# Spacing the transpose banks, moving the sample scores, the first value casts and the last row transposes

## The chip, the cores and the metric

The kernel runs on one core of a Trainium2 chip. The metric is the device time of one execution in microseconds (us). The profile is one execution of the kernel, recorded instruction by instruction; its times are microseconds from the start of the span, which runs from the first to the last instruction.

The engines are named as in the profile: PE is TensorE (matrix multiplications and transposes), DVE is VectorE, ACT is ScalarE, POOL is GpSimd and SP is SyncE, which issues nearly all DMA transfers here.

## What is computed

One step of a decoder layer is computed for 256 new prompt tokens and 8 x 8 sample tokens, 320 columns in all, at a width of 2048: a mixing part (convolution and RWKV-7), then cross-attention into 256 memory tokens, then a gated feed-forward part. The change touches the attention and the very end of the feed-forward part. Cut to these, the reference is:

```python
    h = rms_norm(x, p['norm_xa_pre'])
    q = (h @ p['w_q']).reshape(b_, t_, XA_HEADS, XA_HEAD_DIM)        # 4 heads of 512
    s = jnp.einsum('bthd,bmhd->bhtm', q, mem_k.astype(q.dtype)).astype(jnp.float32) * (XA_HEAD_DIM ** -0.5)
    attn = jax.nn.softmax(s, axis=-1).astype(x.dtype)
    o = jnp.einsum('bhtm,bmhd->bthd', attn, mem_v.astype(x.dtype)).reshape(b_, t_, XA_HEADS * XA_HEAD_DIM)
    x = x + rms_norm(o @ p['w_o'], p['norm_xa_post'])
    ...                                                              # feed-forward, ending in w_down
```

The prompt uses one set of memory keys and values (computed earlier in the kernel), and each of the 8 sample sequences uses its own from a cache: per head, 9 key tiles and 9 value tiles of 256 x 512 float32.

## The kernel before

Products are kept near float32 by splitting each float32 operand into a high and a low float16 part and multiplying three pairs. For each weight tile (`raw`, 512 KB by DMA) ACT makes the high part (`whi`, line 154), DVE the low part (`wlo`, line 155), and PE multiplies (line 57: results `acc`, 128 x 320). A new tile is loaded into one of three `raw` buffers, and there are three `whi` and three `wlo`.

In the attention the kernel works head by head, in two code streams, one for the prompt and one for the samples, which advance between the matmuls of the query weights `w_q` (16 output blocks, four for each head) and of the first columns of the output weights `w_o`:

- A memory tile is loaded into one of five buffers (`rawkv`, line 1176). Keys have to be transposed: PE turns 128 x 128 blocks, four into a PSUM bank (`pk`, line 61), ACT casts the bank to the high part `kh` (line 1245), DVE makes the low part `kl` (line 1246). Values need no transposition: ACT casts the whole tile to `vh` (line 1259), DVE makes `vl` (line 1260).
- The queries leave PSUM on DVE (`qf`, line 1206); ACT and DVE split the prompt's part (`qp`), and ACT and POOL split the samples' part (`qs`, lines 1208, 1211 and 1212).
- The sample scores `pss` use 32-column pieces: four matmuls of 32 columns run side by side on PE, one for each of four sequences. The same is done for the sample outputs `pos`. The prompt's scores and outputs are `psc` and `pav`.
- The softmax takes a maximum on DVE (line 1268), an exponential on ACT (`e`, line 1272), a reciprocal and a scaling on DVE (lines 1273 and 1275). The weights are then turned on PE: `pat` for the prompt, `pas` for the samples; the sample outputs are turned as `pot`.

All of `pk`, `pat`, `pas` and `pot` take a PSUM bank from one group of three (tag `m`), each of which has to be read out by ACT and DVE before it is used again.

What sets the order: the code streams say `yield x` to wait until a planned clock has advanced by x us. That clock is a sum of the planned times of the PE instructions written so far (`mm`, `turn`). So the order is written by the plan, and then a scheduler with its own model of the engines, and priorities, orders each engine's instructions. Loads of memory tiles have a higher priority than the rest of the attention. On the chip every engine runs its instructions in that order and waits on semaphores for what the others have to deliver. The DMA issues on SP stand in one queue in the same way: a load that waits for a buffer holds back the loads behind it.

At the end of the kernel (lines 1540 to 1600) the `w_down` output blocks are scaled on DVE into `mtf` (line 1552) and turned on PE to rows (`pmt`, line 61), while the last `w_down` columns are multiplied from tiles that are held in SBUF (the loop over `held`).

Of the kernel before, what the change touches and what calls it, by code (L numbers as in the profile page):

```python
# [9 lines left out]
F32 = mybir.dt.float32  # L10
# [26 lines left out]
PRI = 3000  # L37
LAT = 1.2
CLAT = 20.0
TAPLAT = 1.18  # L40
KBUF = 8
VBUF = 4
# [4 lines left out]
def hybrid_step_kernel(ctx: ExitStack, tc: tile.TileContext, I, O):  # L47
# [4 lines left out]
    ring = ctx.enter_context(tc.tile_pool(name="ring", bufs=1))  # L52

    clock, pe = [0.0], [None]

    def mm(out, lhsT, rhs, start, stop, skip=False, share=1):
        pe[0] = TE.matmul(out, lhsT=lhsT, rhs=rhs, start=start, stop=stop, skip_group_check=skip)  # L57
        clock[0] += math.prod(rhs.shape[1:]) * (4 if rhs.dtype == F32 else 1) / (2400.0 * share)

    def turn(out, in_, idn):  # L60
        pe[0] = TE.transpose(out, in_, idn)  # L61
        clock[0] += in_.shape[0] / 1200.0

    def late(ins):
        tc.add_manual_dep(ins.ins, pe[0].ins.name, mybir.DependencyInfo(mybir.DependencyClass.NoSync, mybir.DependencyReason.DATA), reason="late")


    ident = cst.tile([P, P], F32, name="ident")
# [1163 lines left out]
    def key_tiles(srcs, h):  # L1232
        t_ = yield from room("k", len(srcs))
        tiles = [[atk.tile([P, 4, NPR], F16, tag=g, bufs=KBUF, name=g) for g in ("kh", "kl")] for _ in srcs]
        raws = [early.pop(n) if n in early else load_kv(src, h, not started) for n, src in srcs]
        started.append(1)
        for raw, (kh, kl) in zip(raws, tiles):
            for z in range(2):
                px = psB.tile([P, 512], F32, tag="m", bufs=3, name="pk")
                for d in range(2):  # L1240
                    for m in range(2):
                        dc = m * 512 + (2 * z + d) * P
                        turn(px[:, d * 256 + m * P:d * 256 + (m + 1) * P], raw[:, dc:dc + P], ident)
                pv = px.rearrange("p (d m) -> p d m", m=NPR)
                A.activation(kh[:, 2 * z:2 * z + 2], pv, AF.Copy, scale=SX)
                V.scalar_tensor_tensor(kl[:, 2 * z:2 * z + 2], pv, SX, kh[:, 2 * z:2 * z + 2], ALU.mult, ALU.subtract)
                yield 0.6
        return tiles, t_

    def value_tiles(srcs, h, kind="v"):  # L1250
        t_ = yield from room(kind, len(srcs))
        tiles = []
        for src in srcs:
            raw = load_kv(src, h)
            if kind == "v":
                vh, vl = (at.tile([P, RING], F16, tag=g, bufs=VBUF, name=g) for g in ("vh", "vl"))
            else:
                vh, vl = (atk.tile([P, 4, NPR], F16, tag=g, bufs=KBUF, name=g).rearrange("p d m -> p (d m)") for g in ("kh", "kl"))
            A.activation(vh, raw, AF.Copy, scale=SX)  # L1259
            V.scalar_tensor_tensor(vl, raw, SX, vh, ALU.mult, ALU.subtract)  # L1260
            tiles.append((vh, vl))
            yield 1
        return tiles, t_

    def softmax(pv, n):

        s = at.tile([P, 4, 2], F32, tag="sst", bufs=2, name="sst")
        V.tensor_reduce(s[:, 0, 0:n], pv, AX.X, ALU.max)
        V.tensor_scalar(s[:, 1, 0:n], s[:, 0, 0:n], -SCL, None, ALU.mult)
        e = at.tile([P, 2, NPR], F32, tag="e", bufs=2, name="e")  # L1270
        for j in range(n):
            A.activation(e[:, j], pv[:, j], AF.Exp, bias=s[:, 1, j:j + 1], scale=SCL, accum_out=s[:, 2, j:j + 1])
        V.reciprocal(s[:, 3, 0:n], s[:, 2, 0:n])
        for j in range(n):
            V.tensor_scalar(e[:, j], e[:, j], s[:, 3, j:j + 1], SA, ALU.mult, ALU.mult)
        return e

    def acc_bank(name):
        return psB.tile([P, 512], F32, tag="acc", name=name)

    def prompt_attention(h):
# [11 lines left out]
        e = softmax(px.rearrange("p (t m) -> p t m", m=NPR), 2)  # L1293
        ((vh, vl),), tv_ = yield from value_tiles([VO], h, "k" if h == 3 else "v")
        yield 3.02
        px = psB.tile([P, 512], F32, tag="m", bufs=3, name="pat")
        for m in range(2):
            for tt in range(2):
# [34 lines left out]
        t_[0] = True  # L1333

    def sample_weights(e, ats):
        px = psB.tile([P, 512], F32, tag="m", bufs=3, name="pas")
        for m in range(2):
            turn(px[:, m * P:(m + 1) * P], e[:, 0, m * P:(m + 1) * P], ident)
        for m in range(2):
            pv = px[:, m * P:(m + 1) * P].rearrange("p (j r) -> p j r", j=4)[:, :, 0:16].rearrange("p j (b e) -> p j b e", b=2)  # L1340
            dh, dl = (ats[:, z, m].rearrange("p j (b e) -> p j b e", e=40)[:, :, :, 0:8] for z in range(2))
            A.activation(dh, pv, AF.Copy)
            V.tensor_tensor(dl, pv, dh, ALU.subtract)
# [11 lines left out]
    def sample_out(h, pos):  # L1355
        os_ = at.tile([P, 512], F32, tag="os", bufs=1, name="os_")
        A.activation(os_, pos, AF.Copy, scale=1.0 / SA)
        yield 0.92
        while oops[h // 2] is None:
            yield 0.5  # L1360
        px = psB.tile([P, 512], F32, tag="m", bufs=3, name="pot")
        for d in range(4):
            turn(px[:, d * P:(d + 1) * P], os_[:, d * P:(d + 1) * P], ident)
        for d in range(4):
            pv = px[:, d * P:(d + 1) * P].rearrange("p (j r) -> p j r", j=4)[:, :, 0:16]
            f = 4 * (h % 2) + d
            dh, dl = (oops[h // 2][:, f, z, 256:320].rearrange("p (j r) -> p j r", j=4) for z in range(2))
            A.activation(dh, pv, AF.Copy)
            V.tensor_tensor(dl, pv, dh, ALU.subtract)
        adone[h] += 1  # L1370
# [14 lines left out]
    def sample_attention():  # L1385
# [4 lines left out]
        for h in range(4):  # L1390
            while qdone[0] < 4 * h + 4:
                yield 0.5
            yield 1.45
            pss = acc_bank("pss")
            sample_scores(h, 0, pss, *kts[h, 0])
            yield 0.21
# [6 lines left out]
            sw_ = spawn(vtiles(h, 1, "k")) if h == 3 else None  # L1403
            kn = spawn(knext(h + 1)) if h < 3 else None
            yield 4.92
            sample_weights(e, atw[h % 2])
            yield 2.2
            (vt,) = yield from join(sv_)
            pos = acc_bank("pos")
# [137 lines left out]
    gpost = vD["norm_ffn_post"]  # L1547
    pt_ = {}

    def turned(f, mi, acc):  # L1550
        z = bw.tile([P, T], F32, tag="qf", name="mtf")
        V.tensor_scalar(z, acc[:, :T], gpost[:, f:f + 1], INV, ALU.mult, ALU.mult)
        for j in range(3):
            if mi == 0:
                pt_[j] = psB.tile([P, 512], F32, tag="m", bufs=3, name="pmt")
            turn(pt_[j][:rows[j], mi * P:(mi + 1) * P], z[:, j * P:j * P + rows[j]], ident)
            if mi == 3 and f < KD - 1:
                A.activation(mtok[j][:, (f - 3) * P:(f + 1) * P], pt_[j][:rows[j]], AF.Copy)

    for _ in project(I["w_down"][0], KF, opn(act), turned, sums[:, 2], (0, 4, 8, 12, 15)):  # L1560
        pass
# [10 lines left out]
    for js, c0, c1 in (((1, 2), P, T), ((0,), 0, P)):  # L1572
        acc = psB.tile([P, 512], F32, tag="acc", name="acc")
        n = c1 - c0
        for kt, ((hi, lo), k) in enumerate(held):
            kc = slice(k * P, (k + 1) * P)
            mm(acc[:, :n], hi[:, kc], act[:, kt, 0, c0:c1], kt == 0, False)
            mm(acc[:, :n], hi[:, kc], act[:, kt, 1, c0:c1], False, False)
            mm(acc[:, :n], lo[:, kc], act[:, kt, 0, c0:c1], False, kt == KF - 1)
# [61 lines left out]
```

## Time and profile before

| quantity | value |
| --- | --- |
| median of 3 runs | 2090.84 us (2090.81 to 2093.16) |
| the profiled execution's own time | 2092.7 us |
| its span, first to last instruction | 2090.9 us |
| mean granted TensorE clock | 0.989 |
| PE busy | 2007.5 us (96% of the span) |
| DVE, ACT, POOL busy | 1396.2, 992.6, 591.9 us |

The profiled execution's time is 1.8 us more than its span, and 1.9 us more than the median. Each row of the profile that names an instruction gives its start, its duration, engine, source line, the operation with what it writes and reads, shape and count; in brackets stands how long the engine sat idle just before, and whose completion ended that. The attention of this section lies between about 871 and 1121 us.

### The profile page before, as it was taken

The numbers are of one execution on the slowest core, as the hardware profiler recorded it, in microseconds if no ns is written. First come the engines' busy times: TensorE is split into PE (matmuls) and PEld (weight loads), VectorE is DVE, ScalarE is ACT, GpSimd is POOL, SyncE is SP. The second block draws the span as 40 slices with busy tenths as digits, with TensorE's granted clock in tenths as the row PEclk, the third lists the DMA queues.
The fourth block names the chain that finished last, engine by engine and source line by source line (L and its number), as shares of the span: only waits on it lengthen the run. The fifth ranks groups of instructions, "written<-read, shape, count | busy, mean of one in ns | idle before, by whom it ended". The sixth has DMA issues, their size and how long they took to land.

```text
span 2090.9 us, 44949 instructions
## 1 busy us (share of the span) xinstructions
PE 2007.5 (96%) x17941; PEld 1393.0 (67%) x17941; DVE 1396.2 (67%) x2479; ACT 992.6 (47%) x1710; POOL 591.9 (28%) x908
## 2 busy tenths in 40 slices
PE   8989999898899999989999999999999999999998
PEld 6756666565454576566677667777777777777777
DVE  5698787986876635977774596666666666444344
ACT  5444445344545544756663454444444444533332
POOL 3635436344022111300001242444444444000000
PEclk9999999999999999999999999999999999999999
DMA  6543334332546765767775445555555555555554
GB/s 188 149 117 101 85 99 112 98 95 65 155 135 208 232 211 176 237 211 243 249 231 162 143 136 163 163 162 163 163 162 162 162 162 162 147 161 162 154 147 144
DMA packets 301998, 333.34 MB, mean 159 GB/s; under 512 B 33882, under 2 KB 227237, under 8 KB 301764
## 3 DMA queue, kind: packets, MB, share of 16 engines
q1 hardware_dynamic: 301788, 330.46, 52.6%
q8 instruction: 141, 2.31, 0.4%
q14 instruction: 69, 0.57, 0.1%
HBM read 319.90 MB, written 11.22 MB: 158 GB/s over the span
## 4 chain that ended last, share of the span: by engine, by line
PE 74%; DVE 11%; DMA 7%; ACT 3%; issue 3%; POOL 2%; SPq 0%; DVEq 0%; POOLq 0%; ACTq 0%
PE acc L57 59%; PE acck L57 5%; DVE wlo L155 3%; DMA rawkv<-in_cache_mem_v_dram 2%; PE pX L57 1%; DVE cvmix L821 1%; ACT whi L154 1%; DVE vl L1260 1%; DMA out_dram<-fo 1%; DMA raw<-in_w_v_dram 1%; PE pk L61 1%; DMA rawkv<-out_dram 1%; DMA raw<-in_w_k_dram 1%; DVE xr L1141 1%; PE psX L57 1%
## 5 line engine op out<-in xcount | busy, mean ns | idle before, releaser
L57 PE MATMUL acc<-h,whi 128*128 128x320 f16 (+1 forms) x4736 | 979.9, 301 | 11.7 <-DVE h L1143 3.7
L155 DVE SCALAR_TENSOR_TENSOR wlo<-raw,whi 128x1024 f16<-128x1024 f32 (+1 forms) x512 | 627.5, 1228 | 473.3 <-ACT whi L154 467.7
L57 PEld LDWEIGHTS <-whi 128*128 128x128 f16 (+1 forms) x7080 | 685.6, 99 | 277.5 <-issue 16.3
L154 ACT ACTIVATE whi<-raw 128x1024 f16<-128x1024 f32 (+1 forms) x512 | 533.0, 1043 | 599.6 <-PE acc L57 497.6
L57 PE MATMUL acc<-h,wlo 128*128 128x320 f16 (+1 forms) x2368 | 701.2, 300 | 0.2 <-DVE wlo L155 0.2
L57 PEld LDWEIGHTS <-wlo 128*128 128x128 f16 (+1 forms) x3540 | 348.4, 98 | 142.4 <-issue 7.1
L57 PE MATMUL acc<-act,whi 128*128 128x320 f16 x1320 | 270.3, 299 | 0.0
L57 PE MATMUL acc<-act,wlo 128*128 128x320 f16 x660 | 196.3, 299 | 0.0
L57 PE MATMUL acck<-whi,memo 128*128 128x512 f16 x512 | 152.6, 383 | 1.3 <-ACT memo L942 1.3
L821 DVE SCALAR_TENSOR_TENSOR cvmix<-GX,cdw,cvmix 128x320 f32<-128x320 f32 x240 | 140.7, 586 | 2.2
L1490 POOL COPY nF<-U 128x9 f32<-128x9 f32 x88 | 50.3, 571 | 302.3 <-DVE U L1489 299.4
L57 PEld LDWEIGHTS <-memo 128*128 128x128 f16 x768 | 72.9, 99 | 83.0 <-issue 4.4
L1487 POOL COPY U<-stF 128x16 f32<-128x16 f32 x88 | 125.9, 1436 | 0.8 <-ACT stF L1475 0.8
L1125 POOL TENSOR_TENSOR sums<-sums,bsq 128x320 f32<-128x320 f32 x33 | 37.9, 1149 | 241.3 <-ACT bsq L1119 239.6
L57 PE MATMUL acck<-wlo,memo 128*128 128x512 f16 x256 | 96.3, 382 | 0.3 <-DVE wlo L155 0.3
L1495 DVE SCALAR_TENSOR_TENSOR C<-U,fdw,C 128x336 f32<-128x336 f32 x176 | 91.8, 564 | 0.0
L1493 ACT ACTIVATE C<-U,fdw 128x336 f32<-128x336 f32 x88 | 56.0, 660 | 34.8 <-DVE U L1489 34.8
L1488 DVE TENSOR_TENSOR U<-acc,rs 128x256 f32<-128x256 f32 x88 | 36.9, 420 | 39.5 <-PE acc L57 39.5
L1260 DVE SCALAR_TENSOR_TENSOR vl<-rawkv,vh 128x1024 f16<-128x1024 f32 x31 | 37.2, 1223 | 30.0 <-ACT vh L1259 29.9
L1211 POOL CAST qs<-qf 128x64 f16<-128x64 f32 x16 | 10.0, 623 | 161.1 <-ACT qf L1208 161.1
L57 PE MATMUL acc<-oopb,whi 128*128 128x320 f16 x256 | 53.7, 299 | 1.0 <-DVE oopb L191 1.0
L57 PE MATMUL acc<-cvmix,whi 128*128 128x320 f16 x256 | 52.1, 299 | 1.5 <-ACT memo L942 1.5
(466 smaller groups left out, 2519.4 us busy)
## 6 DMA issues: line engine op xcount, KB each, us to landing
raw<-in_w_up_dram SPq DMA_DIRECT2D x352, 256.0 KB
raw<-in_w_down_dram SPq DMA_DIRECT2D x71, 512.0 KB
raw<-in_w_in_dram SPq DMA_DIRECT2D x52, 512.0 KB
raw<-in_w_in_dram SPq DMA_DIRECT2D x64, 256.0 KB
raw<-in_w_k_dram SPq DMA_DIRECT2D x32, 512.0 KB
raw<-in_w_v_dram SPq DMA_DIRECT2D x32, 512.0 KB
raw<-in_w_out_dram SPq DMA_DIRECT2D x32, 512.0 KB
rawkv<-in_cache_mem_k_dram SPq DMA_DIRECT2D x32, 512.0 KB
```

What stands on the lines that cost most here:

```text
L57: pe[0] = TE.matmul(out, lhsT=lhsT, rhs=rhs, start=start, stop=stop, skip_group_check=skip)
L61: pe[0] = TE.transpose(out, in_, idn)
L154: A.activation(hi[:, :n], raw[:, :n], AF.Copy, scale=SW)
L155: V.scalar_tensor_tensor(lo[:, :n], raw[:, :n], SW, hi[:, :n], ALU.mult, ALU.subtract)
L821: late(V.scalar_tensor_tensor(o_, i_, cdw[:, c, j:j + 1], o_, ALU.mult, ALU.add))
L1125: (V if f > 11 else G).tensor_tensor(ssum, ssum, sq, ALU.add)
L1260: V.scalar_tensor_tensor(vl, raw, SX, vh, ALU.mult, ALU.subtract)
L1487: G.tensor_copy(us[:, :, 0:2], stF[:, :, :, j])
L1488: V.tensor_tensor(U[:, 2:258], acc[:, 0:256], rf[:, 0:256], ALU.mult)
L1490: G.tensor_copy(nF[:, :, 0, j], U[:, 256:338:10])
L1493: A.activation(c, U[:, 0:336], AF.Identity, bias=fdw[:, 3, j:j + 1], scale=fdw[:, 0, j:j + 1])
L1495: V.scalar_tensor_tensor(c, U[:, t_:t_ + 336], fdw[:, t_, j:j + 1], c, ALU.mult, ALU.add)
```

## The change

There are four edits.

1. A function `bank()` and a number `BANKLAT = 0.9`: a stream that is about to take a bank of the group of three for `pk`, `pat`, `pas` or `pot` waits until the planned clock is 0.9 us beyond the last such use.
2. The sample scores of a head wait 3.6 instead of 1.45 us of the planned clock behind the head's last query block.
3. The casts `vh` of head 0 may not stand ahead of the matmul that was written 24 matmuls earlier. This is a rule on the order alone; no semaphore goes with it.
4. The row transposes of output blocks 13 and 14 of `w_down` are put on a list, and written when the loop over the held tiles is at tile 14.

```diff
+BANKLAT = 0.9
...
+    past_pe = []
     def mm(out, lhsT, rhs, start, stop, skip=False, share=1):
+        past_pe.append(pe[0])
         pe[0] = TE.matmul(out, lhsT=lhsT, rhs=rhs, start=start, stop=stop, skip_group_check=skip)
...
-    def late(ins):
-        tc.add_manual_dep(ins.ins, pe[0].ins.name, mybir.DependencyInfo(mybir.DependencyClass.NoSync, mybir.DependencyReason.DATA), reason="late")
+    def late(ins, n=0):
+        tc.add_manual_dep(ins.ins, (past_pe[-n] if n else pe[0]).ins.name, mybir.DependencyInfo(mybir.DependencyClass.NoSync, mybir.DependencyReason.DATA), reason="late")
...
             for z in range(2):
+                yield from bank()
                 px = psB.tile([P, 512], F32, tag="m", bufs=3, name="pk")
...
-            A.activation(vh, raw, AF.Copy, scale=SX)
+            cast = A.activation(vh, raw, AF.Copy, scale=SX)
+            if h == 0:
+                late(cast, 24)
...
+    bank_at = [0.0]
+
+    def bank():
+        while clock[0] < bank_at[0]:
+            yield bank_at[0] - clock[0] + 0.01
+        bank_at[0] = clock[0] + BANKLAT
...
         yield 3.02
+        yield from bank()
         px = psB.tile([P, 512], F32, tag="m", bufs=3, name="pat")
...
     def sample_weights(e, ats):
+        yield from bank()
         px = psB.tile([P, 512], F32, tag="m", bufs=3, name="pas")
...
+        yield from bank()
         px = psB.tile([P, 512], F32, tag="m", bufs=3, name="pot")
...
-            yield 1.45
+            yield 3.6
             pss = acc_bank("pss")
...
-            sample_weights(e, atw[h % 2])
+            yield from sample_weights(e, atw[h % 2])
...
     def turned(f, mi, acc):
         z = bw.tile([P, T], F32, tag="qf", name="mtf")
         V.tensor_scalar(z, acc[:, :T], gpost[:, f:f + 1], INV, ALU.mult, ALU.mult)
-        for j in range(3):
...
+        def turn_rows():
+            for j in range(3):
...
+        if f < 13:
+            turn_rows()
+        else:
+            waiting.append(turn_rows)
...
             if kt == 14:
+                while waiting:
+                    waiting.pop(0)()
```

The order on ACT at the start of the attention: `vh<-rawkv` are the casts of the first memory values, `whi<-raw` those of the query weights. Before:

```order
L1259 ACTIVATE vh<-rawkv 128x1024
L154 ACTIVATE whi<-raw 128x1024 x3
L1259 ACTIVATE vh<-rawkv 128x1024 x2
L154 ACTIVATE whi<-raw 128x1024 x3
L1259 ACTIVATE vh<-rawkv 128x1024
```

After (the lines of the changed kernel are numbered 3 or 4 higher here):

```order
L157 ACTIVATE whi<-raw 128x1024 x7
L193 ACTIVATE qp<-qf 128x256
L1211 ACTIVATE qf<-qf 128x64
L193 ACTIVATE qp<-qf 128x256
L157 ACTIVATE whi<-raw 128x1024
```

Four value casts stood between the query weight casts, and now none does; the first `vh` stands behind the first head's `kh`.

The order on PE where the sample scores of head 1 begin: `acc<-h,whi` and `acc<-h,wlo` are the last matmuls of the head's query weights, `pss` the scores, `qs` the samples' queries. Before:

```order
L57 MATMUL acc<-h_11283,whi 128x320
L57 LDWEIGHTS wlo
L57 MATMUL acc<-h_11283,wlo 128x320
L57 LDWEIGHTS qs_9806
L57 MATMUL pss<-kh,qs_9806 32x256
```

After, with the matmuls of the query weights 49 rows further up, ahead of 11 `pk` and 19 `pav`, of which these are the last:

```order
L64 MATMUL pk<-ident,rawkv 128x128
L60 LDWEIGHTS vh
L60 MATMUL pav<-al,vh 128x256
L60 LDWEIGHTS vh
L60 MATMUL pav<-al,vh 128x256
L60 LDWEIGHTS qs_9806
L60 MATMUL pss<-kh,qs_9806 32x256
```

The scores followed the query weights at once, and now key transposes and prompt outputs of head 0 stand between.

The order on PE between the end of head 0 and head 1, where turned key blocks (`pk`), prompt weights (`pat`) and sample outputs (`pot`) take the banks. Before:

```order
L57 MATMUL acc<-h_11283,wlo 128x320
L61 MATMUL pk<-ident,rawkv 128x128 x4
L61 MATMUL pot<-ident,os__12326 128x128 x4
L61 MATMUL pk<-ident,rawkv 128x128 x8
L61 MATMUL pat<-ident,e 128x128 x4
L61 MATMUL pk<-ident,rawkv 128x128 x4
L57 LDWEIGHTS vh
L57 MATMUL pav<-ah,vh 128x256
```

After:

```order
L64 MATMUL pk<-ident,rawkv 128x128 x8
L60 LDWEIGHTS ats_9807
L60 MATMUL pos<-vl,ats_9807 32x512
L64 MATMUL pk<-ident,rawkv 128x128
L60 LDWEIGHTS ats_9807
L60 MATMUL pos<-vh,ats_9807 32x512
L64 MATMUL pk<-ident,rawkv 128x128
L60 LDWEIGHTS ats_9807
L60 MATMUL pos<-vh,ats_9807 32x512
L64 MATMUL pk<-ident,rawkv 128x128
```

Six banks were filled in a row, 24 transposes without anything between; now sample outputs stand singly between the transposes.

## Rows read from the trace of the kernel before

**Rows 1.** The page: busy time of the engines, and the chain that ended last.

```profile
PE 2007.5 (96%) x17941; PEld 1393.0 (67%) x17941; DVE 1396.2 (67%) x2479; ACT 992.6 (47%) x1710; POOL 591.9 (28%) x908
...
PE 74%; DVE 11%; DMA 7%; ACT 3%; issue 3%; POOL 2%; SPq 0%; DVEq 0%; POOLq 0%; ACTq 0%
```

**Rows 2.** Waits of PE, 873 to 1121 us: total us, times, longest us.

```profile
PE acc L57 <- ACT whi L154: 2.6, 1, 2.6
PE acc L57 <- DVE qf L1206: 2.3, 1, 2.3
PE pk L61 <- DVE kl L1246: 2.2, 4, 0.5
PE pss L57 <- DVE qf L1206: 1.9, 2, 0.9
...
PE pss L57 <- POOL qs L1211: 1.6, 2, 0.8
PE acc L57 <- DVE oopb L191: 1.0, 1, 1.0
```

**Rows 3.** Timeline of ACT: start, us, instruction, [idle before it and what ended it].

```profile
897.07 1.06 ACT L1259 ACTIVATE vh<-rawkv 128x1024 f16<-128x1024 f32 x1 [6.71 <-DMA rawkv<-in_cache_mem_v_dram]
898.04 2.93 ACT L154 ACTIVATE whi<-raw 128x1024 f16<-128x1024 f32 x3
```

**Rows 4.** The chain that ended last, 880 to 912 us: start, us, what.

```profile
885.62 3.62 DMA rawkv<-in_cache_mem_v_dram
...
891.96 5.09 DMA rawkv<-in_cache_mem_v_dram
```

**Rows 5.** Timeline of PE, start of the sample scores of head 1.

```profile
963.03 0.40 PE L57 MATMUL pss<-kh,qs 128*32 128x256 f16 x8 [0.94 <-DVE qf L1206]
```

**Rows 6.** Stretches: length, busy (x instructions) by engine, PEclk, DMA share, GB/s.

```profile
944.00:946.00 2.00, 1.31 (x8) 0.83 (x8) 1.57 (x5) 1.46 (x5) 0.00 (x0) 1.00 1.09 358
...
966.00:968.00 2.00, 2.00 (x39) 1.37 (x31) 0.92 (x1) 2.00 (x4) 0.00 (x0) 0.50 0.91 312
968.00:970.00 2.00, 2.00 (x26) 1.12 (x24) 2.00 (x4) 0.51 (x2) 0.00 (x0) 0.67 0.40 129
...
1022.00:1024.00 2.00, 2.00 (x37) 0.94 (x31) 1.87 (x3) 1.56 (x4) 0.00 (x0) 0.51 0.58 203
1042.00:1076.00 34.00, 34.00 (x345) 25.56 (x345) 29.14 (x41) 24.16 (x41) 4.37 (x7) 1.00 0.99 326
```

**Rows 7.** Timeline of PE, turned blocks between heads 0 and 1.

```profile
943.99 0.66 PE L61 MATMUL pk<-ident,rawkv 128*128 128x128 f32 x4 [0.54 <-DVE kl L1246]
944.87 0.66 PE L61 MATMUL pat<-ident,e 128*128 128x128 f32 x4 [0.22 <-DVE kl L1246]
```

**Rows 8.** Timeline of PE, a single sample output, and eight together.

```profile
985.92 0.30 PE L57 MATMUL acc<-h,whi 128*128 128x320 f16 x1
986.14 0.39 PE L57 MATMUL pos<-vh,ats 128*32 128x512 f16 x1
986.47 0.31 PE L57 MATMUL acc<-h,whi 128*128 128x320 f16 x1
986.61 0.30 PE L57 MATMUL acc<-h,wlo 128*128 128x320 f16 x1
...
989.33 0.60 PE L57 MATMUL pos<-vh,ats 128*32 128x512 f16 x5
...
989.87 0.55 PE L61 MATMUL pk<-ident,rawkv 128*128 128x128 f32 x3
```

**Rows 9.** Timeline of DVE and PE at the softmax of head 1's samples.

```profile
973.54 1.23 DVE L1260 SCALAR_TENSOR_TENSOR vl<-rawkv,vh 128x1024 f16<-128x1024 f32 x1 [2.91 <-ACT vh L1259]
...
975.74 0.68 DVE L1268 TENSOR_REDUCE sst<-psc 128x2 f32<-128x512 f32 x1
975.88 0.33 PE L61 MATMUL pas<-ident,e 128*128 128x128 f32 x1 [0.22 <-DVE e L1275]
```

**Rows 10.** Timeline of PE, the row transposes of the last output blocks.

```profile
2065.28 0.52 PE L61 MATMUL pmt<-ident,mtf 128*128 128x128 f32 x3 [1.57 <-DVE mtf L1552]
```

More of the change, by code (lines that the diff above doesn't have):

```diff
@@ L1548, in hybrid_step_kernel @@
     pt_ = {}
+    waiting = []
     def turned(f, mi, acc):
@@ L1552, in turned @@
         V.tensor_scalar(z, acc[:, :T], gpost[:, f:f + 1], INV, ALU.mult, ALU.mult)
-        for j in range(3):
[L1554 to L1558, printed above, removed]
+        def turn_rows():
+            for j in range(3):
+                if mi == 0:
+                    pt_[j] = psB.tile([P, 512], F32, tag="m", bufs=3, name="pmt")
+                turn(pt_[j][:rows[j], mi * P:(mi + 1) * P], z[:, j * P:j * P + rows[j]], ident)
+                if mi == 3 and f < KD - 1:
+                    A.activation(mtok[j][:, (f - 3) * P:(f + 1) * P], pt_[j][:rows[j]], AF.Copy)
+        if f < 13:
+            turn_rows()
+        else:
+            waiting.append(turn_rows)
     for _ in project(I["w_down"][0], KF, opn(act), turned, sums[:, 2], (0, 4, 8, 12, 15)):
@@ L1575, in hybrid_step_kernel @@
         for kt, ((hi, lo), k) in enumerate(held):
+            if kt == 14:
+                while waiting:
+                    waiting.pop(0)()
             kc = slice(k * P, (k + 1) * P)
```

## The prediction

> **What bounds the kernel now.** I read the page first. TensorE is busy 96% of the span, and 74% of the chain that ended last is its own work [rows 1]. So a change pays only where TensorE stands still, where its clock is down, or where its work itself grows or shrinks. The second view is the list of TensorE's waits in the attention, since three of the four edits are there. The waits that these edits aim at add up to 2.6 + 2.3 us (first values), 1.9 + 1.6 us (sample scores) and 2.2 us (banks) [rows 2], some 11 us of a 250 us stage. The reader should then look at each place in the timeline: what was late, and what the engine does right behind it. Third come the stretches with the granted clock, because a wait can cost twice: behind the score waits the clock falls to half for a while [rows 6].
>
> **First values (edit 3).** ACT stood idle for 6.71 us ahead of a value cast whose load was on its way, and the three query weight casts behind it began only at 898.04 [rows 3]. TensorE waited 2.6 us for them, and another 2.3 us at the next such place [rows 2]. In the new order seven query weight casts stand in a row and no value cast among them, so nothing on ACT can hold them back but their own loads. I take both waits as gone: 4.9 us. The cast that is moved pulls its DVE half and the load behind it along: a value buffer is now freed later, and on SP's queue the following value loads are issued later. That is counted below.
>
> **Sample scores (edit 2).** At heads 1 and 2 the scores came directly behind the last query weights, and waited 0.94 us for DVE [rows 5], and then for POOL's cast: 1.9 + 1.6 = 3.5 us over both heads [rows 2]. From 966 us on the granted clock was 0.50 and then 0.67 of full speed, so 1.2 GHz for a part of it, directly after those waits; the two stretches lose 2.0 x 0.50 + 2.0 x 0.33 = 1.7 us, and head 2 shows the like, 0.51 [rows 6]. In the new order 11 key transposes and 19 prompt outputs stand between, some 3.3 us of TensorE work at 0.11 us each, more than the waits. So 3.5 + 2 x 1.7 = 6.9 us goes.
>
> **Banks (edit 1).** Between heads four key banks waited 2.2 us in all [rows 2], and the weight bank 0.22 us at each of two heads [rows 7]: 2.6 us. The spacing removes the runs of six banks, and with them these waits.
>
> Each wait also has a refill that its bracket leaves out. From 943.99 to 944.87 lie 0.88 us; four transposes, which start 0.11 us apart, take 0.44 of it and the wait 0.22, so 0.22 is left [rows 7]. Twelve waits of these three kinds make 2.6 us. Gains: 4.9 + 6.9 + 2.6 + 2.6 = 17.0 us. The lower end, with the refills kept and one of the two clock stretches, is 12.7 us.
>
> On the banks a rule of the skill can be held against the trace. At 944 to 946 TensorE is busy only 1.31 of 2.00 us, stopped again and again by banks, and the granted clock is 1.00 [rows 6]. The Trainium skill (TensorE: Matmul & The Clock Gate, section "A second HAM failure mode: psum-queue depth-cycling") says that cycling through PSUM banks makes TensorE idle in small pieces often enough that its clock swings between the half and the full rate. By that rule edit 1 would win clock as well; the trace disagrees here, so by it there is nothing to win and the sum has no such term.
>
> **Last row turns (edit 4).** The order of TensorE, DVE and ACT at the end of the kernel is the same before and after, row for row: the scheduler had already put the transposes there. So the wait of 1.57 us [rows 10] stays, and the edit is worth nothing. If it did act, 1.6 us would be the most.
>
> **What the change costs TensorE: pieces.** The 32-column matmuls only pay in packs of four. A single sample output takes 986.14 to 986.47 plus 0.08 us by which the matmul ahead of it is stretched (0.22 us where 986.47 to 986.61 is the usual 0.14): 0.41 us. Eight together take 0.54 us, 989.33 to 989.87 [rows 8]; so a round of four is 0.22 us, and each piece costs some 0.19 us at its edges. In the new order the bank spacing lets turned key blocks in between: the sample outputs stand in 45 pieces instead of 26, and need 73 rounds instead of 61; the scores stand in 19 pieces instead of 7 (rounds of half the columns, 0.11 us, four more). That is 12 x 0.22 + 19 x 0.19 = 6.2 us and 4 x 0.11 + 12 x 0.19 = 2.7 us, together 9.0 us after rounding. All of it is on TensorE, so all of it is on the path. Lower end 4.5 us, if half of the edges lie in time that TensorE has to wait anyway.
>
> **What it costs in new waits.** Three places in the new order are tight.
> First, the sample weights of head 1. Before, 21 matmuls of the query weights (21 x 0.14 = 2.9 us) stood between the prompt's scores and `pas`, and it still waited 0.22 us for the softmax [rows 9]. In the new order nothing stands there, and on DVE a prompt maximum of 0.68 us and a value half of 1.23 us [rows 9] come ahead of the scaling. So 0.2 to 3.1 us; I take 2.3, near the upper end, since the DVE queue got longer and not shorter.
> Second, the values of head 1. A load takes 3.62 to 5.09 us [rows 4], the cast 1.06 [rows 3]: 4.7 to 6.2 us from issue to use. In the new order one tile's load is released by the low half of the tile ahead of it, and TensorE has 3.3 us of work until it needs it: 1.4 to 2.9 us. Part of it is covered by the stop ahead of it; I take 1, and 1 more for the same thing at heads 0 and 2.
> Third, the end of head 3. Query weights now run ahead: 24 memory tiles are loaded behind the last query weight tile, and before it was 9. The last three value loads follow each other through their casts: 3 x (3.62 to 5.09) + 3 x 1.06 + 2 x 1.23 = 16.5 to 20.9 us, against 16.5 us of TensorE work; and behind the last cast an exponential of the prompt waits on ACT. So 0 to 6 us; I take 4, and the wait of 1.0 us that is there now [rows 2] goes, 3 net.
> Together 2.3 + 1 + 1 + 3 = 7.3 us; ends 1 and 15 (all three at their upper ends and the clock down once more).
>
> **Sum.** -17.0 + 9.0 + 7.3 = -0.7 us. The profiled execution took 2092.7 us, 1.8 us more than its span, and the median of the runs is 2090.84 us; the edits act inside the span, so I move the median by the sum: 2090.1 us, said as 2090.
>
> **Rivals.**
> *The new waits do not come.* Loads may land as early as now, since DMA is not full in most of the stage (share 0.40 to 0.91 around 966 us [rows 6]). Then only 1 us of new waits is left: -17.0 + 9.0 + 1 = -7 us, 2084 us. Against it speaks that the issue order on SP puts values later.
> *Values just in time, slower than before.* At 1042 to 1076 us the DMA share is 0.99 at 326 GB/s [rows 6], so 24 tiles of 512 KB behind the last query weights take at least 24 x 1.6 = 38 us, and any backlog shows at head 3. With new waits of 14 us in place of 7.3: -17.0 + 9.0 + 14 = +6 us, 2097 us. It decides when the new waits exceed 12.2 us, where the sum passes +4.2.
> *The half clock stays.* In place of the pause there is now a stretch of transposes and small matmuls ahead of and among the scores, and the clock may fall there instead. Then 3.4 us of the gain is missing: 2090.8 - 0.7 + 3.4 = 2093.5 us. At 944 to 946 us the same kinds of work ran at 1.00 [rows 6], which speaks against. The Trainium skill (TensorE: Matmul & The Clock Gate, section "Part 4: PE-mode transpose") says that transposes do not count as activity for the clock in the way that matmuls do; by that rule this rival would be the likelier one.
>
> **How the numbers follow.** Forecast 0.40, with a range of its own of 2086 to 2094; no new waits 0.30; just in time 0.22; half clock 0.08. A measurement of this kernel can tell about 0.2%, 4.2 us, from no change. Faster by more (under 2086.7): 0.28 of the second case and 0.05 of the first, 0.33. Slower by more (over 2095.0): 0.20 of the third and 0.03 of the others, 0.23. The same: 0.44. The ends of the unknown terms are -17.0 + 4.5 + 1 = -11.5 us and -12.7 + 9.0 + 15 = +11.3 us; both at once are unlikely, and 8 times in 10 I expect 2081 to 2097.
>
> **What would show it.** In the changed kernel's profile: no wait of `acc` for `whi` or `qf` at the first head (edit 3); no wait of `pss`, and the granted clock at 1.00 around the scores of heads 1 and 2 (edit 2); `pk` and `pat` without waits between heads (edit 1); the 1.57 us wait of `pmt` unchanged (edit 4); single `pos` matmuls 0.3 to 0.4 us apart from what follows; new waits of `pas` at head 1 and of `pos` and `psc` at the end of head 3. I am wrong if the attention gets shorter by more than 6 us, which means that the new waits are hidden, or longer by more than 6 us, which means that loads or the softmax set the pace.

## The result and the profile after

The changed kernel took 2107.07 us (median of 4 runs, 2103.4 to 2108.04) beside 2090.82 us of the kernel before: a ratio of 1.0072 (95% interval 1.0055 to 1.0090). In a later comparison it took 2101.56 us (10 runs) beside 2091.0, a ratio of 1.0045 (1.0030 to 1.0060). It is slower, by some 9 to 16 us. The forecast was 2090 with a range up to 2097, so it missed.

The page of the changed kernel, where [rows 1] showed the one before, has a TensorE that is busy for 8 us more:

```profile
span 2105.7 us, 44934 instructions
...
PE 2015.8 (96%) x17941; PEld 1393.9 (66%) x17941; DVE 1398.4 (66%) x2479; ACT 992.8 (47%) x1710; POOL 588.8 (28%) x908
```

To see where the time went, I laid TensorE's instructions of the attention end to end with the durations that the trace shows for each kind (0.136 us for a 320 column matmul, 0.11 for a transpose or a 256 column matmul, 0.11 for a round of four score matmuls, 0.22 for a round of four sample outputs, 0.19 for each piece of these). I call that the work; what the stretch lasts beyond it I call stops, and these hold the waits, their refills and the half clock. The prices of the pieces are those of the forecast, so the column of the work does not test them. The stretch begins with a run of 63 query matmuls, the same in all kernels, and ends ahead of a run of 112 output matmuls.

| kernel | pieces against before, us | memory loads behind the last query weight | length of the stretch, us | work, us | stops, us | time, ratio to before (95%) |
| --- | --- | --- | --- | --- | --- | --- |
| before | 0 | 9 | 245.6 | 220.0 | 25.6 | 1 |
| full change | +8.9 | 24 | 258.0 | 229.0 | 29.0 | 1.0072 (1.0055 to 1.0090) |
| full change, again | +8.9 | 24 | 258.7 | 229.0 | 29.7 | 1.0045 (1.0030 to 1.0060) |

The two profiles of the full change differ by 0.7 us in this stretch, but the two profiles of another kernel (edits 1 and 3 at 0.6, below) differ by 2.7 us, so 2 or 3 us between single profiles show little. The 12.4 us of the stretch are most of the 14.8 us by which the span grew; 0.5 us lies ahead of it and 1.9 us behind, for which I have no cause. TensorE's order ahead of the stretch is the same in all kernels here, and yet in their profiles the stretch begins anywhere from 865.3 to 873.8 us (873.8 and 868.8 in the two of the full change): part of the spread of the times has nothing to do with the change. Work accounts for 9.0 us, and the stops did not fall but rose by 3.4. These are the waits of TensorE in the changed kernel (total us, times, longest us), to be held against [rows 2]:

```profile
PE pas L64 <- DVE e L1281: 4.2, 1, 4.2
PE pos L60 <- ACT ats L1357: 2.4, 2, 1.8
PE psc L60 <- DVE kl L1250: 2.4, 2, 1.7
PE pav L60 <- ACT ah L1316: 1.8, 3, 0.8
PE psc L60 <- ACT kh L1249: 1.3, 1, 1.3
PE pk L64 <- DMA rawkv<-in_cache_mem_k_dram: 1.3, 1, 1.3
PE pk L64 <- DVE kl L1250: 1.0, 1, 1.0
```

The waits of `acc` for `whi` and `qf` are gone, and those of `pss` for `qf` and `qs`. The bank waits are down to 1.0 us. In their place stand the sample weights `pas`, the prompt's scores `psc` and the sample outputs `pos`, none of which waited for more than 0.3 us in all before.

**Pieces.** The timeline of TensorE in the changed kernel (start, us, instruction) where six banks had stood in a row:

```profile
943.92 0.39 PE L60 MATMUL pos<-vl,ats 128*32 128x512 f16 x1
944.24 0.33 PE L64 MATMUL pk<-ident,rawkv 128*128 128x128 f32 x1
944.50 0.39 PE L60 MATMUL pos<-vh,ats 128*32 128x512 f16 x1
944.82 0.33 PE L64 MATMUL pk<-ident,rawkv 128*128 128x128 f32 x1
945.08 0.39 PE L60 MATMUL pos<-vh,ats 128*32 128x512 f16 x1
945.40 0.33 PE L64 MATMUL pk<-ident,rawkv 128*128 128x128 f32 x1
```

One pair of a single output and a single transpose takes 0.58 us (943.92 to 944.50). Packed, the same two take 0.07 and 0.11 [rows 7, 8]. Four such pairs cost 1.6 us more than they would packed, with no wait in them.

**The sample weights of head 1.** The timeline of ACT in the changed kernel, and then that of TensorE:

```profile
977.06 1.06 ACT L1263 ACTIVATE vh<-rawkv 128x1024 f16<-128x1024 f32 x1 [2.66 <-DMA rawkv<-in_cache_mem_v_dram]
978.02 0.46 ACT L1278 ACTIVATE e<-pss,sst 128x256 f32<-128x256 f32 x1
```

```profile
979.98 0.66 PE L64 MATMUL pas<-ident,e 128*128 128x128 f32 x2 [4.17 <-DVE e L1281]
```

ACT held a value cast `vh` whose tile was still on its way, and the exponential `e`, whose scores were ready, stood behind it. The timeline of DVE shows the rest:

```profile
975.12 0.14 DVE L1275 TENSOR_SCALAR sst<-sst 128x1 f32<-128x1 f32 x1
...
978.15 1.22 DVE L1266 SCALAR_TENSOR_TENSOR vl<-rawkv,vh 128x1024 f16<-128x1024 f32 x1 [1.61 <-ACT vh L1263]
979.29 0.15 DVE L1279 RECIPROCAL sst<-sst 128x1 f32<-128x1 f32 x1
```

The maximum of the scores was there at 975.26 us and the exponential began at 978.02: 2.8 us in ACT's queue. The exponential's sum was there at 978.57, and the value's low half `vl` kept the reciprocal until 979.29: 0.7 us in DVE's. TensorE waited 4.17 us in all. Then the granted clock fell, as stretches of the changed kernel show (length, busy and instructions of PE, PEld, DVE, ACT and POOL, granted clock, DMA share, GB/s):

```profile
978.00:980.00 2.00, 0.02 (x1) 0.05 (x1) 1.69 (x4) 0.96 (x5) 0.00 (x0) 0.93 0.00 0
980.00:982.00 2.00, 2.00 (x10) 1.95 (x10) 0.91 (x4) 1.32 (x6) 0.00 (x0) 0.50 0.69 194
982.00:984.00 2.00, 2.00 (x12) 0.94 (x11) 1.51 (x3) 1.76 (x4) 0.00 (x0) 0.72 0.69 220
...
1086.00:1088.00 2.00, 0.56 (x3) 0.41 (x3) 2.00 (x5) 0.44 (x1) 0.00 (x0) 0.50 1.06 406
1088.00:1090.00 2.00, 2.00 (x12) 1.40 (x10) 1.48 (x2) 1.86 (x5) 0.00 (x0) 0.50 0.23 86
1090.00:1092.00 2.00, 2.00 (x10) 1.29 (x9) 1.92 (x5) 0.71 (x1) 0.00 (x0) 0.50 0.00 0
```

The half clock left the scores of heads 1 and 2 and came back behind the new waits, at 980 and from 1084 on. And while TensorE waited at 978 to 980, the DMA share was 0.00: the next load was issued at 979.40, when `vl` had freed its buffer, and that cast had waited in its queue.

**The end of head 3.** The chain of work in the changed kernel (start, us, what):

```profile
1050.06 10.12 DMA rawkv<-in_cache_mem_k_dram
...
1070.10 4.03 DMA rawkv<-in_cache_mem_v_dram
...
1074.21 1.06 ACT vh L1263
...
1075.30 1.24 DVE vl L1266
1076.54 0.02 issue
1076.56 3.56 DMA rawkv<-in_cache_mem_v_dram
1080.12 0.02 issue
1080.14 1.07 ACT vh L1263
...
1082.37 0.32 DVE kl L1250
```

Load, high half, low half, load, high half: each frees the buffer for the next. The prompt's key halves `kl` that TensorE needed were queued behind these casts. From the last sample scores (1082 us) to the end of the stretch the stops add up to 9.6 us, and to 7.7 in the second profile; before they had 2.3 us there.

**Last row turns.** `pmt` waits as before, 1.68 us where [rows 10] has 1.57:

```profile
2080.01 0.52 PE L64 MATMUL pmt<-ident,mtf 128*128 128x128 f32 x3 [1.68 <-DVE mtf L1570]
```

### The profile page after: what moved, and what is told of

Its sections match the earlier page's. It is cut to its first block, busy times and chain, and to the rows that moved or that the text cites. A ratio compares the mean times of both kernels' runs of the same rounds, so it can differ in the third digit from the quotient of the medians.

```text
span 2105.7 us, 44934 instructions
## 1 busy us (share of the span) xinstructions
PE 2015.8 (96%) x17941; PEld 1393.9 (66%) x17941; DVE 1398.4 (66%) x2479; ACT 992.8 (47%) x1710; POOL 588.8 (28%) x908
## 4 chain that ended last, share of the span: by engine, by line
PE 47%; DVE 2%; DMA 2%; issue 1%; ACT 1%; POOL 0%; DVEq 0%; POOLq 0%; ACTq 0%
PE acc L60 44%; DMA rawkv<-in_cache_mem_v_dram 1%; DMA rawkv<-in_cache_mem_k_dram 0%; DMA raw<-in_w_down_dram 0%; DVE xr L1144 0%; DVE wlo L158 0%; PE pos L60 0%; PE pk L64 0%; DVE h L1146 0%; DMA out_dram<-fo 0%; DVE rz L1143 0%; PE pxt L64 0%; PE pmt L64 0%; PE pav L60 0%; PE pss L60 0%
## 5 line engine op out<-in xcount | busy, mean ns | idle before, releaser
L60 PE MATMUL acc<-rwmix,whi 128*128 128x320 f16 x256 | 52.6, 299 | 0.0
```

## The experiments

Theory A said that the bank spacing makes the loss, theory B that the later scores make the new waits. Each edit by itself first, and the change without the spacing. (Edit 4 leaves the order of every engine at the end of the kernel unchanged and was not run alone; the first three kernels leave it out, all others keep it.)

```diff
 # edit 1 alone
+BANKLAT = 0.9
+                yield from bank()
 # edit 2 alone
-            yield 1.45
+            yield 3.6
 # edit 3 alone
+            if h == 0:
+                late(cast, 24)
 # the full change without the spacing
-BANKLAT = 0.9
+BANKLAT = 0.0
```

> Edit 1 alone: the bank spacing of 0.9, everything else as before. By the count of pieces the sample outputs stand in 51 pieces instead of 26 and the scores (with those at the start) in 33 instead of 15, which makes 13 us of TensorE work; the bank waits of 2.6 us with their refills go. Theory A (the bank spacing makes the loss: its pieces, and by spreading the code also the late loads): at least +10 us, 2101, and with new waits like those of the full change up to 2115. Theory B (moving the scores makes the new waits, the spacing costs its pieces alone): +9 to +11 us, 2100 to 2102, without long new waits.

> Edit 2 alone: the sample scores 3.6 instead of 1.45 us behind the last query block. No pieces (0.05 us). Theory A: the score waits and their half clock go, 7 to 8.6 us: 2082 to 2084. Theory B: the later scores let the query weights run ahead of the memory loads and the new waits of 20 us come with this edit: 2100 to 2103.

> Edit 3 alone: the value casts of head 0 behind the query weight casts. Pieces 1.2 us. Both theories: the two waits of 4.9 us at the first head go, net -4 us: 2087; with late loads at heads 0 and 1 up to 2091.

> The full change without the bank spacing (spacing number 0). Pieces -0.4 us. Theory A: the gains of edits 2 and 3 stay, 5 + 8 us, and the loss is gone: 2077 to 2080. Theory B: pieces are gone but the new waits stay: 2090 to 2098.

| kernel | pieces | loads behind | length | work | stops | ratio |
| --- | --- | --- | --- | --- | --- | --- |
| edit 1 alone | +13.0 | 22 | 277.9 | 233.0 | 44.8 | 1.0162 (1.0130 to 1.0194) |
| edit 2 alone | +0.1 | 17 | 251.6 | 220.4 | 31.2 | 1.0018 (1.0000 to 1.0036) |
| edit 3 alone | +1.2 | 11 | 249.3 | 221.5 | 27.7 | 1.0017 (0.9998 to 1.0037) |
| without spacing | -0.4 | 19 | 253.7 | 220.0 | 33.7 | 1.0039 (1.0020 to 1.0057) |

Edit 1 alone costs more than twice what the full change does: 13.0 us of pieces as counted, and 19 us of stops. Theory A is right that it is the worst edit, though the 2124.91 us lie beyond A's 2115, and B's limit of 11 us falls. But A is wrong too: without the spacing nothing was gained, 2098.81 us where A had 2077 to 2080 and B up to 2098. Edits 2 and 3 alone missed as well: 2095.30 us where A had 2082 to 2084 and B 2100 to 2103, and 2094.98 us where both had 2087 to 2091. Each of the two removes the wait that it aims at and gets another. Edit 2 alone has no wait of `pss` left, and these (total us, times, longest us) in its place:

```profile
PE pk L64 <- DVE kl L1250: 5.9, 5, 4.0
PE acc L60 <- ACT whi L157: 2.8, 1, 2.8
PE pos L60 <- ACT vh L1263: 2.4, 1, 2.4
PE acc L60 <- DVE oopb L1383: 2.4, 3, 1.3
```

The bank waits that [rows 2] showed with 2.2 us have become 5.9. Edit 3 alone has no wait for `whi` or `qf` left, and the banks wait 4.9 us:

```profile
PE pk L64 <- DVE kl L1250: 4.9, 3, 2.6
PE psc L60 <- ACT kh L1249: 3.5, 2, 2.3
```

Both together without spacing: 9.3 us of bank waits. So the spacing meets a real wait that the other edits make worse, and pays for it with pieces and late loads. Edit 1 alone shows the stop of `pas` twice. ACT sat idle for 3.5 and 3.2 us there ahead of a value cast that waited for its load; the second time it was the maximum on DVE that stood behind that cast and its low half, and not the exponential on ACT:

```profile
PE pas L64 <- DVE e L1279: 10.8, 2, 6.6
```

Next the cause of the new waits: theory Q (ACT's queue, a value cast ahead of the exponential) against theory L (the loads come too late anyway); then a smaller spacing, and the change without edit 3.

```diff
 # exponential first, on the full change: a rule on the order alone
+            if behind is not None:          # behind = the exponential of the head's sample scores
+                tc.add_manual_dep(cast.ins, behind.ins.name, mybir.DependencyInfo(mybir.DependencyClass.NoSync, mybir.DependencyReason.DATA), reason="late")
 # spacing 0.6
-BANKLAT = 0.9
+BANKLAT = 0.6
 # without edit 3
-            if h == 0:
-                late(cast, 24)
```

> The full change, and in addition the value casts of a head may not stand ahead of the exponential of that head's sample scores on ACT (a rule on the order alone). Pieces 7.4 instead of 8.9 us; memory loads behind the last query weight 25 instead of 24, so the loads stay late. Theory Q (the new waits come from ACT's queue: a value cast that waits for its load stands ahead of the exponential): the 4.2 us wait of pas at head 1 and the half clock behind it go, and part of the stop at head 3: 2107 - 1.5 - 5 - 3 = 2097 to 2100. Theory L (the loads come too late, whatever the order on ACT): the wait moves from pas to pos, and the time stays, 2104 to 2107.

> The full change with a bank spacing of 0.6 instead of 0.9. Pieces 0.3 instead of 8.9 us, and 16 memory loads behind the last query weight instead of 24. Theory Q: only the pieces go, and the waits of about 20 us stay: 2098. Theory L: pieces and a good part of the late loads go: 2107 - 8.6 - 7 = 2091, near the kernel without spacing, which took 8 us more than before.

> The full change without edit 3 (value casts of head 0 free). Pieces 6.5 instead of 8.9 us, 23 memory loads behind the last query weight. Both theories: the two waits of 4.9 us at the first head are back, less 2.4 us of pieces: 2107 + 4.9 - 2.4 = 2109 to 2110. If edit 3 is what made bank spacing bearable, 2115 or more.

> The full change with spacing 0.6 and the value casts behind the exponential. Pieces 4.5 us, 20 memory loads behind the last query weight. Theory Q: 2107 - 4.4 - 8 = 2095. Theory L: between the two others by its loads, 2096 to 2102.

| kernel | pieces | loads behind | length | work | stops | ratio |
| --- | --- | --- | --- | --- | --- | --- |
| exponential first | +7.4 | 25 | 252.3 | 227.4 | 25.0 | 1.0037 (1.0018 to 1.0056) |
| spacing 0.6 | +0.3 | 16 | 256.1 | 220.7 | 35.5 | 1.0026 (1.0009 to 1.0044) |
| without edit 3 | +6.5 | 23 | 261.1 | 226.6 | 34.6 | 1.0070 (1.0051 to 1.0089) |
| spacing 0.6, exponential first | +4.5 | 20 | 261.5 | 224.6 | 36.9 | 1.0064 (1.0045 to 1.0083) |

With the exponential first, with as many late loads, the timelines of ACT and of TensorE, and a stretch behind them, show at the same place:

```profile
975.08 0.47 ACT L1282 ACTIVATE e<-pss,sst 128x256 f32<-128x256 f32 x1 [0.95 <-DVE sst L1279]
...
975.55 1.05 ACT L1265 ACTIVATE vh<-rawkv 128x1024 f16<-128x1024 f32 x1
```

```profile
976.87 0.30 PE L64 MATMUL pas<-ident,e 128*128 128x128 f32 x1 [1.33 <-DVE e L1285]
```

```profile
980.00:982.00 2.00, 2.00 (x17) 1.43 (x16) 0.00 (x0) 0.00 (x0) 0.00 (x0) 1.00 0.97 326
```

The wait falls from 4.17 to 1.33 us, the clock stays at 1.00, and the stretch is 6 us shorter, 1.6 of it pieces. That is Q, for this place. At head 3 it is not: Q expected part of that stop gone, and from the last sample scores on there are 11.5 us of stops, beside 9.6 and 7.7 in the full change. The 2098.83 us lie in Q's range, but in the time the gain can't be told from the full change's own spread (1.0037 beside 1.0045 and 1.0072). The smaller spacing removes the pieces, but its bank waits are 10.0 us:

```profile
PE pk L64 <- DVE kl L1250: 10.0, 4, 4.8
```

Its time came out where Q had it, 2098.01, but by luck: the `pas` wait that Q kept is down to 0.6 us, and the bank waits took its place. Its loads were fewer without helping: L's 2091 missed. The two cures together did not add; 2105.73 missed both, with new waits of `pos` for ACT's `ats` (5.6 us) and of `pot` for ACT's `os` (4.6 us). Without edit 3 the wait for `whi` is back (3.1 us), as expected, and the 2107.65 us are near the 2109 to 2110.

Then the end of head 3, with work left out there. The kernel without both was run later, beside the full change; the first two had expectations that start from its first timing.

```diff
 # loads out: the second set's casts read the first set's tiles
+            raw = saved[n] if again else load_kv(src, h)
 # casts out: the second set's loads stay, the first set's cast tiles are used again
+            if again:
+                tiles.append(saved[n])
+                continue
 # both out: neither loads nor casts of the second set
```

> The full change with the second set of sample values of head 3 cast from the tiles of the first set: four loads of 512 KB are left out at the end of the attention, and all casts stay (so the samples of the second set get the values of the first). In the full change the stop at the end of head 3 holds 13 us more than the work, part of it half clock. Theory L (late loads make that stop): 8 to 12 us less, 2095 to 2099. Theory C (the casts that queue on ACT and DVE ahead of the key casts and exponentials make it): at most 3 us less, 2104 to 2107.

> The full change with the second set's casts of head 3 left out and its four loads kept (the first set's cast tiles are used again): four casts of 1.06 us on ACT and four of 1.23 us on DVE go. Theory C: 8 to 12 us less than the full change, 2095 to 2099. Theory L: about 2 us less, 2105.

> The full change as it is, run beside the next kernel for a comparison on the same chip: 1.0072 of the kernel before as at first, 2104 to 2108 where before takes 2090.

> The full change without loads and without casts of the second set of sample values of head 3 (the first set's cast tiles are used again). With the loads left out, or the casts, it was 6.5 us less each, by the ratio. If the stop at the end of head 3 is one chain of loads and casts in turn, of which each of the two cuts a link, both together give about the same, 2096 to 2098; if loads and casts each cost their own part, about 13 us less, 2091 to 2094.

| kernel | length | stops | ratio |
| --- | --- | --- | --- |
| full change, two profiles | 258.0, 258.7 | 29.0, 29.7 | 1.0072, 1.0045 |
| loads out | 256.6 | 27.5 | 1.0041 (1.0026 to 1.0055) |
| casts out | 254.9 | 26.5 | 1.0040 (1.0026 to 1.0053) |
| both out | 253.0 | 24.4 | 1.0029 (1.0014 to 1.0044) |

By the length, against 258.3, the loads were worth 1.8 us, the casts 3.4 and both 5.3. The times, 2098.39, 2097.33 and 2097.87 us, lie in the ranges of L, of C and of the one chain in turn, but these started from 2107, and the full change's second timing of 2101.56 (2104 to 2108 were expected) leaves 3 to 4 us for each; the intervals overlap with it. The place itself says something else than the length. From the last wait of `pav` for `ah` ahead of head 3 (1067.04 us in the full change) to the end of the stretch, the stops are 10.8 and 9.6 us in the full change, 11.1 without the loads, 8.8 without the casts and 6.6 without both. So the loads by themselves were worth nothing there, the casts 1 to 2 us and both 3 to 4. Other waits came for those that went, without the loads a second `pas` wait of 4.2 us, behind casts on ACT and DVE, and without the casts one of `pss` for a key cast:

```profile
PE pas L64 <- DVE e L1287: 8.4, 2, 4.2
```

```profile
PE pss L60 <- ACT kh L1249: 3.3, 2, 3.1
```

Neither theory alone makes this stop, and much of it remains without either (6.6 us, where the kernel before has 2.3 from its last sample scores on); with one profile each, what makes the rest is open.

Last, what in the spacing does the harm. The count of pieces jumps between 0.80 and 0.85. Theory P says that the loss sets in with the order that is written, theory S that it grows with the spacing as such. Edits 1 and 3, without edit 2, at three spacings, one of them with the scores at 2.0; and a spacing of 0.6 alone:

```diff
-            yield 3.6
+            yield 1.45      # 2.0 in one kernel
-BANKLAT = 0.9
+BANKLAT = 0.6              # 0.80, 0.85
```

> Edits 1 and 3 without edit 2, with a spacing of 0.6: pieces 0.2 us, and 9 memory loads behind the last query weight as before. Theory L (the loss goes with pieces and late loads): the waits at the first head go and nothing comes for them, 5 to 7 us less than before: 2084 to 2087. Theory W (whatever moves, other waits take their place, some 25 to 35 us of them in every order): 2090 to 2096, as with edit 3 alone.

> As the run before, with the sample scores 2.0 instead of 1.45 us behind the last query block: pieces 0.8 us, 9 memory loads behind the last query weight. Theory L: 2084 to 2087, a little less if the score waits shrink. Theory W: 2090 to 2096.

> Edits 1 and 3 without edit 2, spacing 0.80: pieces 1.7 us, 11 memory loads behind the last query weight. Theory P (the spacing's loss comes from the order it writes, its pieces and late loads, and sets in with them): near before, 2088 to 2093. Theory S (the loss grows evenly with the spacing, since each bank use is put off): nearly as much as at 0.85 and 0.9, 2105 or more.

> The same with spacing 0.85: pieces 14.0 us, 22 memory loads behind the last query weight, the kinds of numbers that the full change and edit 1 alone have. Theory P: 12.3 us of pieces more than at 0.80 and the waits of late loads on top, 2112 to 2122, a jump of over 20 us for 0.05. Theory S: within 2 us of the kernel with 0.80.

> Edit 1 alone with spacing 0.6: pieces 0 us, 9 memory loads behind the last query weight. Theory P: what is left is the gain of the banks and the 4.9 us waits of the first head stay, 2087 to 2091. Theory S: two thirds of the loss of edit 1 alone, over 2105.

> Edits 1 and 3 with spacing 0.6, run again with more rounds: the trace of the first run shows an attention of 250.1 us instead of 251.5, the first head's waits gone and no pieces. If that holds, 1 to 4 us less than before, 2087 to 2090; if its lower time was the spread of the runs, equal to before.

| kernel | pieces | loads behind | length | work | stops | ratio |
| --- | --- | --- | --- | --- | --- | --- |
| edits 1, 3 at 0.6 | +0.2 | 9 | 244.4 | 220.1 | 24.3 | 0.9990 (0.9978 to 1.0002) |
| the same, again | +0.2 | 9 | 241.7 | 220.1 | 21.6 | 0.9995 (0.9982 to 1.0007) |
| scores at 2.0 | +0.8 | 9 | 243.8 | 220.8 | 23.0 | 1.0003 (0.9988 to 1.0018) |
| at 0.80 | +1.7 | 11 | 245.3 | 222.0 | 23.2 | 1.0041 (1.0027 to 1.0055) |
| at 0.85 | +14.0 | 22 | 272.1 | 234.0 | 38.2 | 1.0139 (1.0117 to 1.0161) |
| edit 1 alone at 0.6 | 0.0 | 9 | 248.7 | 220.0 | 28.8 | 1.0026 (1.0006 to 1.0045) |

From 0.80 to 0.85 the stretch grows by 26.8 us: 11.9 us of work, as the pieces say, and 14.9 us of stops. In the time it is 2098.43 to 2119.16. That is P's jump, and S falls. P's numbers fit less well: 2098.43 is above its 2093, and edit 1 alone at 0.6 took 2097.52, above its 2091. Pieces and late loads turn over together here, so what each of them costs is not told apart; earlier loads with the same pieces were not tried. The longest waits at 0.85 are again `pas` for the exponential and `pos` for value casts:

```profile
PE pas L64 <- DVE e L1281: 8.5, 2, 5.9
PE pos L60 <- ACT vh L1263: 3.0, 4, 1.5
PE pk L64 <- DMA rawkv<-in_cache_mem_k_dram: 2.8, 1, 2.8
```

Only the kernels at 0.6 with edit 3 and without edit 2's 3.6 (scores at 1.45 or 2.0) shortened the stretch, by 1.2 to 3.9 us; the best of them ran at 0.9990 and 0.9995, which can't be told from the kernel before. Of the two theories on it, L (2084 to 2087) and W (2090 to 2096), neither has its 2088.89 and 2089.81; at 2.0 the 2090.26 are W's. The waits of the first head are gone, and bank waits of 4.6 and 3.0 us and others have come, as W said, though the stops are 21.6 to 24.3 us and not its 25 to 35. The time of the kernel at 0.80 lies 7 us above what its stretch, as long as before, would give. Its profile has 6.3 us more than the one before behind the stretch, some 3 of them at the very end, where the granted clock falls behind a wait of 1.99 us of the row transposes `pmt`:

```profile
2066.00:2068.00 2.00, 2.00 (x16) 1.91 (x17) 0.00 (x0) 0.00 (x0) 0.00 (x0) 0.50 0.00 0
```

That profile is the fastest of its seven executions, so whether the others lose the same, I don't know. No version beat the kernel before clearly.

## Why the prediction was wrong

- **What bounds the kernel** (TensorE, so a change pays in its waits, its clock and its work): right. TensorE is busy for 96% of the span before and after, and the change paid in these three. (That work and stops add up to the stretch says nothing, since the stops are what is left over.)
- **First values, 4.9 us gone**: right. No wait of `acc` for `whi` or `qf` is left, with edit 3 alone as in the full change.
- **Sample scores, 3.5 us of waits and two half clock stretches gone**: right at that place. But the half clock came back behind other waits. The rival "the half clock stays" expected it among transposes and small matmuls; in the changed kernel the stretch of single transposes and outputs runs at full clock,

```profile
944.00:946.00 2.00, 2.00 (x8) 0.73 (x8) 0.03 (x1) 0.95 (x1) 0.19 (x1) 1.00 1.03 350
```

  with 1.00 granted, and so it does in the second profile. The Trainium skill (TensorE: Matmul & The Clock Gate, section "Part 4: PE-mode transpose") says that transposes do not count as activity for the clock in the way that matmuls do. Neither trace shows a fall among them. But right behind them the second profile has a bank wait of 1.39 us, where the first has one of 0.97, and there the clock fell:

```profile
943.91 0.66 PE L64 MATMUL pk<-ident,rawkv 128*128 128x128 f32 x4 [1.39 <-DVE kl L1250]
```

```profile
946.00:948.00 2.00, 2.00 (x9) 1.10 (x8) 2.00 (x4) 0.92 (x2) 0.00 (x0) 0.50 0.82 250
```

  So a bank wait cost clock once, where the forecast had no such term; whether the transposes ahead of it had a part, these two profiles can't tell.
- **Banks, 2.6 us gone**: about half; 1.0 and 0.3 us are left (1.4 and 0.3 in the second profile). What the forecast missed is that edits 2 and 3 make the bank waits larger (4.9, 5.9 and 9.3 us without spacing), so that the edits can't be costed one by one from the kernel before.
- **Pieces, 9.0 us**: about right. The 9.0 us of work rest on the same 0.19 us a piece and are no test. Prices that are taken from all the traces instead, as the median time from one start to the next for each pair of neighbours without a wait, make 10.2 us, since a piece costs about 0.20 us between matmuls and 0.25 between transposes. The stops then grow by 2 to 3 us and not by 3.4. The lower end of 4.5 us, with half of the edges in waits, did not come true: 4 of the 63 pieces have a wait at their start and 3 right behind.
- **Last row turns, nothing**: right.
- **New waits, 7.3 us**: this step failed. Of the 17.0 us of gains some 15 came, so of 25.6 us of stops 10.6 should be left; there were 29.0, so the new ones are about 18 us. The first place had 2.3 us, and took 4.2 us and the half clock. The step bounded it by the matmuls that no longer stood ahead of it (3.1 us) and looked at DVE's queue, which held it for 0.7 us; what held it for 2.8 us was ACT's queue, where a value cast with 2.66 us still to wait for its tile stood ahead of the exponential. The second place had 2 us, and showed one wait of 0.5 (`pos` for `vh`). The third place had 4 us, and took 9.6 us with half clock: I set three loads against 16.5 us of work, and left out that the key casts that TensorE needs first stand behind the value casts on ACT and DVE. With four loads and their casts taken out, 6.6 of some 10 us were left, so the size of this stop is measured and its cause is shown only in part. The rest, some 4 us in pieces of about 1 us, had no term.
- **The rival "values just in time"** is the nearest: slower, by late values and a stop at the end of head 3. Its price, 14 us of new waits, was too low. Its cause, a full DMA, is not what the trace shows at head 1: at 978 to 980 us the DMA share is 0.00 while TensorE waits. There the queue's order holds the casts, the casts hold the buffers, and the buffers hold the loads. At head 3 the DMA was all but full for a time: the share is 0.93 to 1.06 from 1050 to 1062 us, where the key load of 10.12 us ran, and TensorE waited 1.3 us for it.

## What to carry to other kernels

Where engines run fixed queues and are busy for much of a stage (before: TensorE 236, DVE 182 and ACT 149 of 252 us), a removed wait is worth nothing until the new order of every queue behind it has been read: look for an instruction that waits on a load ahead of one that the bound engine needs soon. Count what a new order does to work that only pays in packs, since that part of the cost can be read closely before any run (9.0 us forecast, 10.2 by the traces). And when a planning number is raised, step through its values: here the written order, and 20 us with it, turned over between 0.80 and 0.85. Last, look for the gain of an experiment at the place that it is about: leaving out four loads made the stretch 1.8 us shorter, and none of it at the stop that they were to explain.

## What the runs showed of the hardware that was not expected

A single 32-column matmul between two transposes costs TensorE 0.47 us of its 0.58 us pair, where a packed one costs 0.07. The clock fell to 0.50 behind single waits of 4.17 us (`pas`, at 980) as it had behind two of 0.94 and 0.79 us (the scores, at 966), and not behind the 1.33 us wait of `pas` in the kernel with the exponential first. But it fell behind a bank wait of 1.39 us in the second profile of the full change. And the length of a wait does not settle it: at the end of the kernel it fell behind a `pmt` wait of 1.99 us (at 0.80), and not behind one of 2.05 (edits 1 and 3 at 0.6, again). That kernel's first profile has two stretches at 0.50 in the attention and its second none, with the same order of TensorE and 2.7 us between the two. The same pair of kernels gave 1.0072 and 1.0045 in two comparisons, while the changed one's attention took 258.0 and 258.7 us; the length of a stretch leaves out the spread of what lies ahead of it, but not that of its own waits and clock.
